# A trunk's last activation pair, first gate weights and final gate in another order

## The chip, the cores and the metric

One core of one Trainium2 chip. The metric is the device time of the whole program in microseconds (us). The engines are TensorE (PE, with its weight loads as PEld), VectorE (DVE), ScalarE (ACT), GpSimd (POOL) and SyncE (SP), which issues most of the DMAs. Each engine works its instructions in the order in which they stand in the program, and waits on semaphores where an instruction needs what another engine or a DMA made.

## The reference, cut to what matters

Two layers over 512 tokens of width 1024. Each layer has a token mixer (not touched here), a squared-ReLU MLP and a gated per-layer embedding; a last norm follows.

```python
for i in range(DEPTH):                     # DEPTH = 2
    hn = rmsnorm(h, norm_mix_g[i])
    h = h + mixer(hn)                      # even: stick-breaking + differential; odd: dilated windows
    hn = rmsnorm(h, norm_mlp_g[i])
    u = jnp.square(jax.nn.relu(hn @ w_mlp_up[i]))
    h = h + u @ w_mlp_down[i]
    gate = jax.nn.sigmoid(rmsnorm(h, norm_ple_g[i]) @ w_ple_gate[i])
    h = h + (p[i] @ w_ple_proj[i]) * gate
return rmsnorm(h, final_norm_g)
```

## The kernel before

**Products.** Every fp32 operand is split into a high part, written by ACT as fp32r (`wh`, `hi`, `uh`), and a low part, the rest, written by DVE or POOL (`wl`, `lo`, `ul`). A product is three matmuls: high by high, high by low, low by high (`mm3`, lines 137 to 142). h is kept transposed in eight tiles of 128 x 512.

**Weights.** `wload` has SP bring 1 MB into `raw` (two buffers), `wsplit` makes the two parts of half a load (128 x 1024 each, lines 117 to 129) in a ring of three buffers, or four in a pool that is handed in. A load can start only when both halves of the load before last have been split.

**The MLP** (line 711). `up(ch, c)` makes two accumulators of 24 matmuls each (512 columns), then for the pair: relu times norm on DVE (L738), square on ACT (L739), three differences on DVE (L744 to L748), and the split of all seven quarters `u` into `uh` (L750) and `ul` (L751), since the down product is done by a scheme with seven products of half size. In the last chunk of four an additional split of one quarter goes to `spare` (L742, L743). `down(ch, c)` makes sums of the weight's quarters (`s13`, `s24`), splits them (L789, L790), and runs its products over the four pairs k = 0 to 3. The first down unit of the last chunk, `down(3, 0)`, takes k = 0 to 2 of all its products ahead of k = 3, as pair 3 comes last. Its weight splits are w13, w24, w11 and, inside the products, w for A12 and A22.

The side sums of a unit (L888) read what a POOL DMA has accumulated (`side`). `nxt.done(k)` then scales and splits an h tile for the gate's norm and adds its squares to `rstd`: by DVE (L254), or for the first tiles by an accumulating DMA of POOL's (L247). `down_last(3)` is the last down unit, in plain form: two accumulators of 36 matmuls.

**The gate.** In layer 0 `ple_t` (line 915) takes four loads of `w_gate`, each with two blocks; for the first load it alternates the two accumulators over k. In layer 1 `ple_final` (line 933) works in two halves of the columns, each with four weight blocks b = 0 to 3 from two loads, and four token tiles t. In the first half b is the outer loop, with the transposes of h between (`turn`, L943, DVE's copies L944) and the norm: `norm.finish()` sums `rstd` over the partitions by two matmuls (L261, L262), then Ln (L210) and Exp (L213) on ACT, three steps on DVE (L214 to L216), four transposes (L284) and `rcol` (L286). In the second half t is outer. Each tile has a sigmoid (L994), product (L995), addition (L996) and the sum of squares (L997); after the first half POOL multiplies by the final norm's weights (L999). After a tile's second half, thirteen small DVE steps (L1003 to L272) make its scale; ACT (L950) and DVE (L952) apply it and SP writes the tile out.

**What sets the order.** The program's text gives a priority, and a scheduler places the instructions of each engine by it and by its own costs, so that each engine's order differs from the text. `order(later, earlier)` (line 224) binds two instructions without a semaphore of its own.

## Time and profile before

| | us |
|---|---|
| median of three runs | 1305.18 |
| lowest, highest | 1303.14, 1307.39 |
| the profiled execution, own time | 1305.36 |
| its span, first to last instruction | 1303.6 |
| PE busy in the span | 1277.1 (98%) |
| DVE, ACT, POOL busy | 1005.1, 710.2, 213.2 |
| granted TensorE clock, mean | 0.996 |

Times in the rows below count from the first instruction; layer 0 ends near 640. A matmul row's end is modelled and overlaps the next one's start, so the spacing of the starts is its cost. A waiting instruction shows in brackets how long its engine was idle ahead of it, and who released it. A row that ends in x2 or x3 is several instructions in one stretch.

### The profile page before, as it was taken

To read this page: it belongs to the slowest core of one execution; us is meant where nothing else is said; L and a number is where in the kernel's file an instruction comes from. 1 tells how busy PE (TensorE), PEld (TensorE's weight loads), DVE (VectorE), ACT (ScalarE), POOL (GpSimd) and SP (SyncE) were. 2 spreads that over 40 slices of the span, in tenths; PEclk is the share of its full clock that TensorE was granted. 3 is DMA by queue.
4 is the path that set the end of the run, shared out by engine and by line. 5 is a ranking of instruction groups with operands and counts; after the bars stand their busy time and mean duration, and the time that the engine had idled before them with its cause. 6 is when DMAs were issued, how large, how long until landed. Compare 5 with 4: busy or idle time off the path is not lost.

```text
span 1303.6 us, 19326 instructions
## 1 busy us (share of the span) xinstructions
PE 1277.1 (98%) x7520; PEld 1125.7 (86%) x7520; DVE 1005.1 (77%) x1673; ACT 710.2 (54%) x1149; POOL 213.2 (16%) x184
## 2 busy tenths in 40 slices
PE   9999999999999999999999999999999999999996
PEld 7988887888988989988889888788899898998975
DVE  6788798778858869679767777887785885976876
ACT  6666867555535344355456666764553433534644
POOL 2433533400000000001023333231000000000201
PEclk9999999999999999999999999999999999999998
DMA  6421423222232322646432222212323133254741
GB/s 213 140 81 61 151 74 113 89 98 97 98 99 96 117 103 77 189 116 172 173 130 82 81 89 82 65 58 97 101 94 129 65 103 124 85 163 141 170 145 65
DMA packets 33996, 144.25 MB, mean 111 GB/s; under 512 B 3889, under 2 KB 4625, under 8 KB 21233
## 3 DMA queue, kind: packets, MB, share of 16 engines
q1 hardware_dynamic: 29680, 135.16, 30.6%
q0 software_dynamic: 4224, 7.87, 3.5%
q8 instruction: 59, 0.97, 0.3%
q14 instruction: 33, 0.26, 0.1%
HBM read 131.92 MB, written 6.37 MB: 106 GB/s over the span
## 4 chain that ended last, share of the span: by engine, by line
PE 76%; DVE 11%; ACT 5%; DMA 4%; issue 3%; POOL 0%; SPq 0%; ACTq 0%; DVEq 0%; POOLq 0%
PE mm L138 11%; PE mm L142 10%; PE mm L141 10%; PE sc L141 5%; PE sc L142 5%; PE sc L138 5%; PE pv L142 4%; PE pv L141 4%; PE pv L138 4%; PE tp L142 4%; PE tp L141 4%; PE tp L138 4%; PE pv L558 3%; PE tp L539 2%; DMA side<-u 2%
## 5 line engine op out<-in xcount | busy, mean ns | idle before, releaser
L122 ACT ACTIVATE wh<-raw 128x1024 fp32r<-128x1024 f32 (+1 forms) x156 | 160.5, 1034 | 142.7 <-PE mm L141 47.9
L126 POOL TENSOR_TENSOR wl<-raw,wh 128x512 fp32r<-128x512 f32 (+1 forms) x132 | 178.3, 1373 | 304.1 <-ACT wh L122 304.1
L138 PE MATMUL mm<-hi,wh 128*128 128x512 f32 x472 | 187.1, 396 | 0.2 <-ACT pjt L372 0.2
L142 PE MATMUL mm<-hi,wl 128*128 128x512 f32 x472 | 185.0, 392 | 1.6 <-DVE wl L128 1.5
L141 PE MATMUL mm<-lo,wh 128*128 128x512 f32 x472 | 184.6, 391 | 0.0
L128 DVE TENSOR_TENSOR wl<-raw,wh 128x1024 fp32r<-128x1024 f32 x90 | 109.4, 1221 | 46.4 <-ACT wh L122 40.8
L142 PEld LDWEIGHTS mm<-hi,wl 128*128 128x128 f32 x472 | 88.6, 188 | 22.2 <-DVE wl L128 2.2
L138 PEld LDWEIGHTS mm<-hi,wh 128*128 128x128 f32 x472 | 88.7, 188 | 16.8 <-ACT pjt L372 0.4
L141 PEld LDWEIGHTS mm<-lo,wh 128*128 128x128 f32 x472 | 88.8, 188 | 15.6
L760 POOL DMA_DIRECT2D s<-in_w_down_dram x4 | 4.5, 1123 | 579.1 <-DMA s<-in_w_down_dram 313.2
L789 ACT ACTIVATE wh<-s 128x1024 fp32r<-128x1024 f32 x58 | 61.1, 1053 | 52.8 <-DVE s L776 14.7
L751 DVE TENSOR_TENSOR ul<-u,uh 128x1792 fp32r<-128x1792 f32 x32 | 64.8, 2024 | 31.9 <-ACT uh L750 31.8
L533 ACT ACTIVATE e<-e,mn 128x128 f32<-128x128 f32 (+3 forms) x96 | 53.8, 561 | 62.3 <-DVE mn L530 61.9
L790 DVE TENSOR_TENSOR wl<-s,wh 128x1024 fp32r<-128x1024 f32 x58 | 70.8, 1221 | 13.9 <-ACT wh L789 13.5
L750 ACT ACTIVATE uh<-u 128x1792 fp32r<-128x1792 f32 x32 | 54.5, 1703 | 48.4 <-DVE u L748 48.2
L739 ACT ACTIVATE u<-u 128x512 f32<-128x512 f32 x64 | 39.7, 626 | 68.0 <-DVE u L738 67.8
L141 PE MATMUL sc<-lo,wh 128*128 128x512 f32 x184 | 72.1, 392 | 0.3 <-DVE lo L183 0.3
L138 PE MATMUL sc<-hi,wh 128*128 128x512 f32 x184 | 72.2, 392 | 0.1
L142 PE MATMUL sc<-hi,wl 128*128 128x512 f32 x184 | 71.9, 391 | 0.0
L138 PE MATMUL mm<-wh,hi 128*128 128x256 f32 (+1 forms) x216 | 63.2, 292 | 0.0
L142 PE MATMUL mm<-wh,lo 128*128 128x256 f32 (+1 forms) x216 | 62.9, 291 | 0.0
L141 PE MATMUL mm<-wl,hi 128*128 128x256 f32 (+1 forms) x216 | 62.8, 291 | 0.0
(305 smaller groups left out, 3887.1 us busy)
## 6 DMA issues: line engine op xcount, KB each, us to landing
raw<-in_w_up_dram SPq DMA_DIRECT2D x32, 1024.0 KB, 4.9
raw<-in_w_down_dram SPq DMA_DIRECT2D x32, 1024.0 KB, 4.9
raw<-in_w_in_dram SPq DMA_DIRECT2D x23, 1024.0 KB, 4.9
raw<-in_w_gate_dram SPq DMA_DIRECT2D x8, 1024.0 KB, 6.0
bias<-urow SPq DMA_DIRECT2D x24, 256.0 KB, 3.6
raw<-in_w_outa_dram SPq DMA_DIRECT2D x8, 768.0 KB, 4.2
pj<-pjd SPq DMA_DIRECT2D x16, 256.0 KB, 5.7
h<-in_xT_dram SPq DMA_DIRECT2D x8, 256.0 KB, 5.7
```

The lines of the kernel that those rows point to most:

```text
L122: nc.scalar.activation(hi, src, AF.Copy)
L126: nc.gpsimd.tensor_tensor(lo[:, kx], src[:, kx], hi[:, kx].bitcast(F32), op=ALU.subtract)
L128: nc.vector.tensor_tensor(lo, src, hi.bitcast(F32), op=ALU.subtract)
L138: mm = nc.tensor.matmul(acc, lh, rh, start=start, stop=False)
L141: nc.tensor.matmul(acc, lh, rl, start=False, stop=False)
L142: return mm.ins, nc.tensor.matmul(acc, ll, rh, start=False, stop=stop).ins
L533: nc.scalar.activation(e[:, 0:n], e[:, 0:n], AF.Exp, scale=-1.0, bias=mn, accum_out=s)
L739: nc.scalar.activation(ui, ui, AF.Square, scale=0.5)
L750: nc.scalar.activation(uh, u, AF.Copy)
L751: part = nc.vector.tensor_tensor(ul, u, uh.bitcast(F32), op=ALU.subtract)
L789: nc.scalar.activation(hi, src, AF.Copy)
L790: low[:] = [nc.vector.tensor_tensor(lo, src, hi.bitcast(F32), op=ALU.subtract).ins]
```

## The change

It has three parts.

1. In `down(3, 0)` of both layers, the low part of w24 is bound behind the last pair's first relu, the high part of A12/A22 behind its second square, and that block's low part behind its last difference.
2. In `down_last` the first load of the gate is asked for, and split, after the first accumulator's matmuls in the text. The side sums of the unit before are bound behind the first block's low part, and the `rstd` additions of its two tiles behind the second's. `ple_t` and `ple_final` take these blocks over.
3. In `ple_final` the fourth block of the first half comes from the pool handed in, not the ring, and the last block of the second half from the ring. The high and low parts of the last load are bound behind the norm's Exp and its last step. `tok_cols` stands later, after the second token tile of b = 3.

```diff
 def wsplit(raw, i, nk, n, pool=None):
...
-            nc.vector.tensor_tensor(lo, src, hi.bitcast(F32), op=ALU.subtract)
+            last_low[:] = [nc.vector.tensor_tensor(lo, src, hi.bitcast(F32), op=ALU.subtract).ins]
+        last_high[:] = [act.ins]
...
 def rsqrt(...):
+        root[:] = [ex.ins, nc.vector.scalar_tensor_tensor(y, t, 3.0 / scale, y, op0=ALU.subtract, op1=ALU.mult).ins]
...
 Norm.stats:
+                add = nc.vector.tensor_tensor(self.acc, self.acc, sq, op=ALU.add)
+                for a in late_add:
+                    order(add.ins, a)
...
 up:
+                chain.append(nc.vector.scalar_tensor_tensor(ui, acc, 0.0, rstd[0], op0=ALU.max, op1=ALU.mult).ins)
+                chain.append(nc.scalar.activation(ui, ui, AF.Square, scale=0.5).ins)
...
-            hidden[ch, c] = (uh, ul, part.ins)
+            hidden[ch, c] = (uh, ul, part.ins, chain[0], chain[3], t4.ins)
...
 down:
             w24 = split(s24)
+            if last and c == 0:
+                order(low[0], hidden[ch, 3][3])
...
                     w = split(rv[:, A12:A22 + 1])
+                    if last and c == 0:
+                        order(high[0], hidden[ch, 3][4])
+                        order(low[0], hidden[ch, 3][5])
...
 down_last:
-            low.clear()
             defer = []
-            finished(c - 1)
...
+                if i == 0:
+                    raw = wload(w_gate[layer, 0])
+                    n = (KT, P) if layer < DEPTH - 1 else (2, 512)
+                    gate.append(wsplit(raw, 0, *n))
+                    low[:] = last_low
+                    gate.append(wsplit(raw, 1, *n))
+                    late_add[:] = last_low
+                    finished(c - 1)
...
 ple_t:
-            blk = block(w_gate[layer, c], KT, P)
+            blk = gate if c == 0 else block(w_gate[layer, c], KT, P)
...
 ple_final:
-            gw = []
-            for half in range(2):
+            gw = [] if c else list(gate)
+            for half in range(1 - c, 2):
                 raw = wload(w_gate[layer, 2 * c + half])
                 for b in range(2):
-                    gw.append(wsplit(raw, b, 2, 512, pool=fpool if c else None))
+                    gw.append(wsplit(raw, b, 2, 512, pool=None if (c, half, b) in ((0, 1, 0), (1, 1, 1)) else fpool))
+                    if c and half:
+                        order(last_high[0], root[0])
+                        order(last_low[0], root[1])
...
                         contract(t, b, 0)
+                        if b == 3 and t == 1:
+                            rcol = tok_cols(rstd)
...
-                        rcol = tok_cols(norm.finish())
+                        rstd = norm.finish()
                         turn(1)
```

The diff as printed is cut and its hunks are named by function. How the scheduler placed the instructions shows in each engine's order. Line numbers of the changed kernel are its own.

**DVE at the end of the last `up` of layer 1.** `u_11905` is the last pair, `wl_11946` the low part of w24, `wl_11999` that of A12/A22. Before:

```order
L790 TENSOR_TENSOR wl_11946<-s_2147_11930,wh_11945 128x1024
L738 SCALAR_TENSOR_TENSOR u_11905<-pv_11855,rstd_9229 128x512
L743 TENSOR_TENSOR spare_11753<-u_11905,spare_11753 128x256
L738 SCALAR_TENSOR_TENSOR u_11905<-pv_11856,rstd_9229 128x512
L790 TENSOR_TENSOR wl_11999<-raw_11927,wh_11998 128x1024
L744 TENSOR_TENSOR u_11905<-u_11905 128x2x256
L746 SCALAR_TENSOR_TENSOR u_11905<-u_11905 128x256
L748 SCALAR_TENSOR_TENSOR u_11905<-u_11905 128x256
L751 TENSOR_TENSOR ul_11907<-u_11905,uh_11906 128x1792
```

In the changed kernel, the same stretch of DVE:

```order
L748 SCALAR_TENSOR_TENSOR u_11905<-pv_11855,rstd_9229 128x512
L800 TENSOR_TENSOR wl_11946<-s_2147_11930,wh_11945 128x1024
L753 TENSOR_TENSOR spare_11753<-u_11905,spare_11753 128x256
L748 SCALAR_TENSOR_TENSOR u_11905<-pv_11856,rstd_9229 128x512
L754 TENSOR_TENSOR u_11905<-u_11905 128x2x256
L756 SCALAR_TENSOR_TENSOR u_11905<-u_11905 128x256
L758 SCALAR_TENSOR_TENSOR u_11905<-u_11905 128x256
L800 TENSOR_TENSOR wl_11999<-raw_11927,wh_11998 128x1024
L761 TENSOR_TENSOR ul_11907<-u_11905,uh_11906 128x1792
```

Each low part moved down, past one relu and past the three differences. On ACT the high part of A12/A22 moved behind the second square; layer 0 reads the same.

**DVE around the last down unit of layer 0.** `side_3071` and `side_3072` are the sums of the third unit, `wl_6195` and `wl_6199` (before) or `wl_6100` and `wl_6104` (now) the gate's first two low parts. Before:

```order
L888 TENSOR_TENSOR side_3071<-side_3071,side_3072 128x256
L128 TENSOR_TENSOR wl_6195<-raw_6192,wh_6194 128x1024
L888 TENSOR_TENSOR h_97<-h_97,side_3071 128x256
...
L254 TENSOR_TENSOR rstd_5902<-rstd_5902,e_6072 128x512
L873 TENSOR_TENSOR h_99<-h_99,tp_6082 128x512
L183 SCALAR_TENSOR_TENSOR lo_6076<-h_98,gcols,hi_6075 128x512
L254 TENSOR_TENSOR rstd_5902<-rstd_5902,e_6079 128x512
L183 SCALAR_TENSOR_TENSOR lo_6121<-h_99,gcols,hi_6120 128x512
L128 TENSOR_TENSOR wl_6199<-raw_6192,wh_6198 128x1024
```

In the changed kernel, from the same place of DVE on:

```order
L128 TENSOR_TENSOR wl_6100<-raw_6097,wh_6099 128x1024
L910 TENSOR_TENSOR h_97<-h_97,side_3072 128x256
L910 TENSOR_TENSOR side_3071<-side_3071,side_3072 128x256
...
L894 TENSOR_TENSOR h_99<-h_99,tp_6060 128x512
L128 TENSOR_TENSOR wl_6104<-raw_6097,wh_6103 128x1024
L261 TENSOR_TENSOR rstd_5902<-rstd_5902,e_6119 128x512
L186 SCALAR_TENSOR_TENSOR lo_6123<-h_98,gcols,hi_6122 128x512
```

The first low part moved up past the first two side sums, the second past both `rstd` additions and two `lo`. In layer 1 both moved alike.

**ACT in the final gate.** `raw_12686` and `raw_12696` are the third and fourth load, `rstd_12174` the norm. Before:

```order
L259 ACTIVATE e_12595<-rstd_12174 128x512
L122 ACTIVATE wh_12688<-raw_12686 128x1024
L122 ACTIVATE wh_12490<-raw_12484 128x1024
L122 ACTIVATE wh_12692<-raw_12686 128x1024
L122 ACTIVATE wh_12698<-raw_12696 128x1024
L122 ACTIVATE wh_12702<-raw_12696 128x1024
L210 ACTIVATE rstd_12174<-tp_12594,eps_n 128x512
L213 ACTIVATE rstd_12174<-rstd_12174 128x512
```

In the changed kernel, on ACT:

```order
L122 ACTIVATE wh_12688<-raw_12686 128x1024
L122 ACTIVATE wh_12692<-raw_12686 128x1024
L268 ACTIVATE e_12595<-rstd_12174 128x512
L213 ACTIVATE rstd_12174<-tp_12594,eps_n 128x512
L216 ACTIVATE rstd_12174<-rstd_12174 128x512
L122 ACTIVATE wh_12698<-raw_12696 128x1024
L122 ACTIVATE wh_12702<-raw_12696 128x1024
```

Ln and Exp (the two rows that write `rstd`) moved up past the two high parts of the fourth load; the three others moved ahead of the norm.

**DVE in the final gate's second half.** `fin_12741` and `fin_12742` are the first tile's scale, `gt_12784` and `ht_12477` belong to the second tile. Before:

```order
L272 SCALAR_TENSOR_TENSOR fin_12741<-fin_12742,fin_12741 128x1
L952 SCALAR_TENSOR_TENSOR ht_12466<-ht_12466,fin_12741,gb_12464 128x512
L995 TENSOR_TENSOR gt_12784<-gt_12784,pj_12458 128x512
L996 TENSOR_TENSOR ht_12467<-ht_12467,gt_12784 128x512
L1003 TENSOR_TENSOR fin_12789<-ssq_12471 128x1
```

In the changed kernel, on DVE (four small steps of the scale and the first tile's last step follow):

```order
L281 SCALAR_TENSOR_TENSOR fin_12741<-fin_12742,fin_12741 128x1
L1023 TENSOR_TENSOR gt_12784<-gt_12784,pj_12468 128x512
L279 TENSOR_TENSOR fin_12742<-fin_12741 128x1
L1024 TENSOR_TENSOR ht_12477<-ht_12477,gt_12784 128x512
L280 SCALAR_TENSOR_TENSOR fin_12742<-fin_12742,fin_12740 128x1
```

The second tile's product and addition moved from behind the first tile's scaling to the middle of its small steps; on ACT the second tile's sigmoid moved ahead of the first tile's scaled copy. Ahead of this stretch, `rcol` moved on DVE behind all four copies of the second `turn` and behind the first low part of the fourth load, where it stood ahead of the copies and behind both low parts before.

More of the change, by code (lines that the diff above doesn't have):

```diff
@@ L121, in wsplit @@
         src = raw[:, i * nk * n:(i + 1) * nk * n].rearrange("p (k c) -> p k c", k=nk)
-        nc.scalar.activation(hi, src, AF.Copy)
+        act = nc.scalar.activation(hi, src, AF.Copy)
         if lo_eng[0] is nc.gpsimd:
@@ L127, in wsplit @@
         else:
-            nc.vector.tensor_tensor(lo, src, hi.bitcast(F32), op=ALU.subtract)
+            last_low[:] = [nc.vector.tensor_tensor(lo, src, hi.bitcast(F32), op=ALU.subtract).ins]
+        last_high[:] = [act.ins]
         return hi, lo
+    last_low, last_high = [], []
     def block(src, nk, n):
@@ L212, in rsqrt @@
             order(ln.ins, tables)
-        nc.scalar.activation(y, y, AF.Exp, scale=-0.5)
+        ex = nc.scalar.activation(y, y, AF.Exp, scale=-0.5)
         nc.vector.tensor_tensor(t, y, y, op=ALU.mult)
         nc.vector.scalar_tensor_tensor(t, mean, eps / scale, t, op0=ALU.add, op1=ALU.mult)
-        nc.vector.scalar_tensor_tensor(y, t, 3.0 / scale, y, op0=ALU.subtract, op1=ALU.mult)
+        root[:] = [ex.ins, nc.vector.scalar_tensor_tensor(y, t, 3.0 / scale, y, op0=ALU.subtract, op1=ALU.mult).ins]
+    root = []
     def use_tables(after):
@@ L228, in order @@
             reason="activation tables")
+    late_add, gate = [], []
     class Norm:
@@ L253, in stats @@
             else:
-                nc.vector.tensor_tensor(self.acc, self.acc, sq, op=ALU.add)
+                add = nc.vector.tensor_tensor(self.acc, self.acc, sq, op=ALU.add)
+                for a in late_add:
+                    order(add.ins, a)
         def finish(self, tables=None):
@@ L715, in mlp @@
         sides = [[fpool.tile([P, S], F32, tag=f"side{x}{c}", name=nm("side"), bufs=1) for x in range(2)] for c in range(4)]
-        hidden, spare, stages, b12, low, lows = {}, [], [], [], [], []
+        hidden, spare, stages, b12, low, lows, high = {}, [], [], [], [], [], []
         def up(ch, c):
@@ L735, in up @@
             ul = fpool.tile([P, 7, HW], F32R, tag="ul", name=nm("ul"), bufs=5)
+            chain = []
             for i, acc in enumerate(accs):
                 ui = u[:, B11 + 2 * i:B11 + 2 * i + 2].rearrange("p a c -> p (a c)")
-                nc.vector.scalar_tensor_tensor(ui, acc, 0.0, rstd[0], op0=ALU.max, op1=ALU.mult)
-                nc.scalar.activation(ui, ui, AF.Square, scale=0.5)
+                chain.append(nc.vector.scalar_tensor_tensor(ui, acc, 0.0, rstd[0], op0=ALU.max, op1=ALU.mult).ins)
+                chain.append(nc.scalar.activation(ui, ui, AF.Square, scale=0.5).ins)
             if ch == NCH - 1:
@@ L747, in up @@
                 u[:, T2], u[:, T1], -1.0, u[:, B22], op0=ALU.mult, op1=ALU.subtract)
-            nc.vector.scalar_tensor_tensor(
+            t4 = nc.vector.scalar_tensor_tensor(
                 u[:, T4], u[:, T2], -1.0, u[:, B21], op0=ALU.mult, op1=ALU.subtract)
@@ L788, in split @@
                 src = src.rearrange("p s (k c) -> p s k c", k=4)
-                nc.scalar.activation(hi, src, AF.Copy)
+                high[:] = [nc.scalar.activation(hi, src, AF.Copy).ins]
                 low[:] = [nc.vector.tensor_tensor(lo, src, hi.bitcast(F32), op=ALU.subtract).ins]
@@ L872, in down_last @@
                                                  stop=k == KT - 1 and lh is wl)
+                if i == 0:
[6 more added lines that the diff above has]
+                    finished(c - 1)
                 nc.vector.tensor_tensor(h[2 * c + i], h[2 * c + i], acc, op=ALU.add)
                 nxt.done(2 * c + i, defer=defer)
+            late_add.clear()
         def finished(c):
@@ L921, in ple_t @@
             if c == 0:
+                gate.clear()
                 rstd = norm.finish()
```

## The prediction

> **What bounds the kernel now.** I read the page's chain of work first, then the list of what TensorE (PE) waited for, then the timelines of single engines around those waits.
>
> ```profile
> PE 76%; DVE 11%; ACT 5%; DMA 4%; issue 3%; POOL 0%; SPq 0%; ACTq 0%; DVEq 0%; POOLq 0%
> ...
> PE mm L141 <- DVE ul L751: 2.0, 2, 1.0
> PE tp L284 <- DVE rstd L216: 1.7, 1, 1.7
> ...
> PE mm L142 <- DVE wl L128: 1.5, 1, 1.5
> ```
>
> Three quarters of the chain is matmul, so a microsecond in which PE stands still is a microsecond of the kernel, as long as PE stays the bound afterwards. The list (total, times, longest) names few waits: PE waits for VectorE (DVE) or ScalarE (ACT), and no row of it names a DMA. The change touches three rows: `ul` of the last activation pair (once per layer), the gate's low part (layer 0), and the gate norm's `rstd` (layer 1). The last 35 us are different: there PE is not the bound, see the third part.
>
> **Part 1, the last activation pair (both layers).** Layer 1, DVE first, then ACT, then PE, and PE in layer 0; start, duration, operation, and idle time with its releaser in brackets:
>
> ```profile
> 1195.39 1.22 DVE L790 TENSOR_TENSOR wl<-s,wh 128x1024 fp32r<-128x1024 f32 x1
> 1196.53 0.69 DVE L738 SCALAR_TENSOR_TENSOR u<-pv,rstd 128x512 f32<-128x512 f32 x1
> 1198.42 0.43 DVE L743 TENSOR_TENSOR spare<-u,spare 128x256 fp32r<-128x256 f32 x1 [1.21 <-ACT spare L742]
> ...
> 1199.37 1.23 DVE L790 TENSOR_TENSOR wl<-raw,wh 128x1024 fp32r<-128x1024 f32 x1
> 1200.51 0.69 DVE L744 TENSOR_TENSOR u<-u 128x512 f32<-128x512 f32 x1
> ...
> 1203.94 2.02 DVE L751 TENSOR_TENSOR ul<-u,uh 128x1792 fp32r<-128x1792 f32 x1 [1.83 <-ACT uh L750]
> ```
>
> ```profile
> 1197.97 0.42 ACT L742 ACTIVATE spare<-u 128x256 fp32r<-128x256 f32 x1
> 1198.29 1.04 ACT L789 ACTIVATE wh<-raw 128x1024 fp32r<-128x1024 f32 x1
> 1199.48 0.63 ACT L739 ACTIVATE u<-u 128x512 f32<-128x512 f32 x1
> 1202.21 1.70 ACT L750 ACTIVATE uh<-u 128x1792 fp32r<-128x1792 f32 x1 [2.10 <-DVE u L748]
> ```
>
> ```profile
> 1204.70 0.28 PE L138 MATMUL mm<-uh,wh 128*128 128x256 f32 x1
> 1206.03 0.39 PE L141 MATMUL mm<-ul,wh 128*128 128x256 f32 x1 [1.04 <-DVE ul L751]
> ```
>
> ```profile
> 578.42 0.39 PE L141 MATMUL mm<-ul,wh 128*128 128x256 f32 x1 [0.93 <-DVE ul L751]
> ```
>
> The pair's chain is relu, square, differences, `uh`, `ul`. Two low parts (1.22 and 1.23 us) and one high part (1.04) stand in it. With the new order the first relu takes the place at 1195.39; its square runs 1196.17 to 1196.80 while DVE does the low part (to 1197.2); ACT's `spare` ends at 1197.25, DVE's at 1197.7; the second relu ends at 1198.3, its square at 1199.0. Before, that square ended at 1200.11 and the difference then stood behind a low part until 1200.51; now the difference starts at 1199.05. From there to the start of `ul` the rows give 3.43 us (1200.51 to 1203.94): `ul` starts at 1202.5 and ends at 1204.5, 1.46 earlier.
>
> PE wants it 0.12 (the spacing of its 256-column matmuls, 0.28 less the overlap) after 1204.70, at 1204.82. So the whole wait goes, with 0.3 to spare. It cost 1206.03 - 1204.82 = 1.2, and one stretched matmul (0.39 for 0.28) 0.1 more: **1.3 us in layer 1**, and by its idle time 0.11 less, **1.2 us in layer 0**. What is late next: the low part of A12/A22 moves behind the differences, from 1199.37 to about 1200.6, ending 1201.8. 63 matmuls of 0.12 stand ahead of 1204.70 in its unit, which so starts at 1197.15; PE needs the part in the 48th: 1202.8. That leaves 1.0 us. It also frees `raw` 1.2 us later, but the load into it is for the unit after next, more than a whole unit of matmuls away. Bounds: 0 if the wait only changes its name, 2.5 for both layers together. I take 2.5, since the slack on both sides is from rows of the same operations.
>
> **Part 2, the gate's first weights (layer 0).** DVE, then PE:
>
> ```profile
> 605.95 0.42 DVE L888 TENSOR_TENSOR h<-h,side 128x256 f32<-128x256 f32 x1 [2.37 <-DMA side<-u]
> ...
> 606.62 1.22 DVE L128 TENSOR_TENSOR wl<-raw,wh 128x1024 fp32r<-128x1024 f32 x1
> ...
> 611.45 0.69 DVE L254 TENSOR_TENSOR rstd<-rstd,e 128x512 f32<-128x512 f32 x1 [0.72 <-DMA rstd<-side]
> ...
> 614.58 1.22 DVE L128 TENSOR_TENSOR wl<-raw,wh 128x1024 fp32r<-128x1024 f32 x1
> ```
>
> ```profile
> 613.99 0.40 PE L141 MATMUL mm<-lo,wh 128*128 128x512 f32 x1
> 615.85 0.50 PE L142 MATMUL mm<-hi,wl 128*128 128x512 f32 x1 [1.46 <-DVE wl L128]
> ```
>
> Both low parts are placed by the new order ahead of what DVE waits for: the first before the side sums (2.37 us of idle time hide its 1.22), the second before the `rstd` addition that waits for an accumulating DMA. The second then runs at about 610.1 to 611.3: the side sums lose the low part in their midst (1.1 earlier), and its high part on ACT follows them. PE needs it at 614.2. The wait goes: 615.85 - 614.22 (0.23 is the spacing at 512 columns) = 1.63, and 0.1 of stretched matmul, **1.7 us**. Behind the second low part now queue the additions and `lo` of three h tiles, 1.2 us at most; PE reads those 7 to 10 us after its gate begins (six matmuls of 0.23 a k, from the sixth k on), so nobody waits. In layer 1 the same move removes no wait of PE (none is in the list), but lets `raw` go about 5 us sooner, and with it the third load of the gate. Bounds 0 and 1.8; I take 1.7.
>
> **Part 3, the final gate (layer 1).**
>
> ```profile
> 1253.41 0.66 PE L943 MATMUL tp<-ident,h 128*128 128x128 f32 x4 [0.20 <-DVE ht L944]
> ...
> 1259.39 0.40 PE L261 MATMUL tp<-e,ones_r 128*128 128x512 f32 x1
> ...
> 1265.45 0.63 PE L284 MATMUL tp<-ident,rstd 128*128 128x128 f32 x4 [1.74 <-DVE rstd L216]
> ...
> 1291.60 0.28 PE L142 MATMUL mm<-wh,lo 128*128 128x256 f32 x1
> ```
>
> ```profile
> 1223.87 19.57 SPq L114 DMA_DIRECT2D raw<-in_w_gate_dram  x3
> ...
> 1259.80 2.01 ACT L122 ACTIVATE wh<-raw 128x1024 fp32r<-128x1024 f32 x2 [8.68 <-DMA raw<-in_w_gate_dram]
> 1261.71 0.67 ACT L210 ACTIVATE rstd<-tp,eps_n 128x512 f32<-128x512 f32 x1
> ...
> 1284.20 0.67 ACT L994 ACTIVATE gt<-tp,rcol 128x512 f32<-128x512 f32 x1
> ...
> 1295.02 0.45 ACT L994 ACTIVATE gt<-mm,rcol 128x256 f32<-128x256 f32 x1
> ```
>
> ```profile
> 1266.12 0.16 DVE L286 TENSOR_SCALAR rcol<-tp 128x4 f32<-128x4 f32 x1 [0.81 <-PE tp L284]
> ...
> 1271.99 1.52 DVE L995 TENSOR_TENSOR gt<-gt,pj 128x512 f32<-128x512 f32 x1 [0.18 <-ACT gt L994]
> ...
> 1279.53 0.69 DVE L996 TENSOR_TENSOR ht<-ht,gt 128x512 f32<-128x512 f32 x1
> ...
> 1281.01 0.16 DVE L1003 TENSOR_TENSOR fin<-ssq 128x1 f32<-128x1 f32 x1 [0.79 <-ACT gt L997]
> ...
> 1283.32 0.16 DVE L272 SCALAR_TENSOR_TENSOR fin<-fin,fin 128x1 f32<-128x1 f32 x1
> ...
> 1291.74 0.69 DVE L996 TENSOR_TENSOR ht<-ht,gt 128x512 f32<-128x512 f32 x1
> ```
>
> ```profile
> 1271.33 3.34 POOL L999 TENSOR_TENSOR ht<-ht,gb 128x512 f32<-128x512 f32 x2 [36.29 <-ACT gt L997]
> ```
>
> Now the norm's Ln stands on ACT behind two high parts that wait for the fourth gate load until 1259.80. PE loses 1.74 for it, and 0.3 at the first transposes. With Ln and Exp ahead of the weights, PE begins its second half about 2.0 earlier. But PE is not the bound there: its last matmul ends at 1291.9, and the last sigmoid starts at 1295.02. So the end must be followed on ACT and DVE, in four steps.
> (i) Ln can start when the two sums of L261/L262 are done: 1259.39 - 0.3 + 0.24 + 0.4, near 1259.8; Exp ends at 1261.1. On DVE follow, in the new order, three steps of the norm and three more copies out of PSUM between them (0.69 each), one low part (1.22), then `rcol`: 1261.1 + 6 x 0.69 + 1.22 less the overlaps (0.08 each, as between neighbouring rows) is near 1266.2, no earlier than 1266.12 before.
> (ii) The copies are done by then, so the products for the four token tiles run closer together; POOL's multiplications fall on them. The first tile of the second half is added by 1279.65 where it was 1280.22: 0.6 gained.
> (iii) From there to the third tile's addition, 1292.43 - 1280.22 = 12.2 before, two rounds of square and reading its sum (0.8), thirteen small steps (1281.01 to 1283.48, 0.19 each, 2.5 together), ACT's scaled copy, sigmoid (0.67), product and addition (0.69 each) one after another. In the new order the second tile's sigmoid stands ahead of that copy, and its product and addition inside the small steps: 0.8 + 7 small steps 1.35 + product and addition with two steps 1.4 + the rest 1.0 + DVE's L952 0.75 + 2.5 + 0.75 + 0.69 + 0.69 = 9.9, some 9.7 with overlaps. 2.5 gained.
> (iv) From there the orders of ACT and DVE are equal, and PE (end 1289.9) stays ahead of the last sigmoid (1291.9).
> That makes **3.1 us**. Bounds: 0.6 if (iii) gives nothing; 2.0 + 3.1 = 5.1, if the end hung on PE alone.
>
> The row to weigh is POOL's. Its two multiplications take 3.34; the DVE product that begins 0.66 after them takes 1.52, where the same operation without POOL takes 0.69. By the rows DVE waits out the POOL operation in progress, and (ii) counts it so at all four of them, some 0.8 us each but for the third.
>
> [...]
>
> **Sum.** 1.3 + 1.2 + 1.7 + 3.1 = 7.3 us. The profiled execution took 1305.36 and would take 1298.1; the median shown is 1305.18, 0.18 less, so I forecast **1297.9**. Instructions and bytes stay the same in number. The gate's blocks in other buffers cost nothing that I count: the fourth block no longer waits for the buffer of the first, the last one takes that buffer long after PE has read it, and the transfers that PE and ACT now check for have landed by then (DVE's additions that read them stand ahead of the last h tile).
>
> **Rivals.**
> (A) *The end keeps its old pace*: ACT and DVE stay the bound and step (iii) does not come, as a late sigmoid there pushes the small steps back. For it: the second tile's product stands between steps that other tiles wait for. Against: its sigmoid needs only PE, and PE is 2 us ahead. It gives 4.2 + 0.6, so 1300.4.
> (B) *The wait changes its name in part 1*: PE waits for the A12/A22 low part instead of `ul`. For it: that part starts only after the differences. Against: 1.0 us of slack. The price is 2.5: 1300.4.
> (C) *The gains of layer 0 are lost later*, to something paced by transfers, and the end keeps its pace as well. Against: no DMA in PE's list. 7.3 - 2.9 - 2.5 = 1.9: 1303.3.
> (D) *Slower*: `rcol`, which all sigmoids need, now stands on DVE behind the low part that waits for the fourth gate load. That load landed by 1259.80; now it goes out some 5 us sooner, close behind the third (1 MB), `pj` (2 MB) and `gb` (0.5 MB). It has until 1261.1, the end of Exp; each us later delays the end by one, and beyond 1268.4 the kernel is slower than before.
>
> ```profile
> DMA packets 33996, 144.25 MB, mean 111 GB/s; under 512 B 3889, under 2 KB 4625, under 8 KB 21233
> ```
>
> The third load was issued at 1243.1 (the end of SP's stretch of three, less its 0.33) and goes out near 1237.8 now. At the mean rate of this line the 4.5 MB from there on would take 40 us, to 1278, and the kernel 1315. But the same 4.5 MB went from 1243.1 to 1259.8 before, 16.7 us; at that pace they end at 1254.5.
>
> **How the numbers follow.** Forecast 0.66, (A) 0.14, (B) 0.07, (C) 0.08, (D) 0.05. A measurement of this kernel tells about 0.3% (3.9 us) from no change. Faster by more, below 1301.3: forecast, (A) and (B), less 0.07 for those that a scatter of some us takes over the line: 0.80. Within 0.3%: 0.15. Slower: 0.05. The range of 1295.0 to 1302.0 takes in the forecast with its upper bound (1295.9 less some scatter), (A) and (B), 0.87 less the scatter; (C) and (D) are out.
>
> **What would show it.** Part 1: in both layers no wait of PE for `ul`, and `ul` starting about 1.4 sooner against PE's unit; a wait for `wl` of the same unit in its place is (B). Part 2: no wait for the gate's low part near 614. Part 3: Ln before the last two high parts, no wait for `rstd`, 9.7 us instead of 12.2 between the additions of the first and the third tile, and the last sigmoid some 2 us after PE's end instead of 3.1. Wrong would be: `rcol` later than 1.5 us behind its old place against the gate's start, a PE wait that is new, or a final stage no shorter than before.

## The result, and the profile after

| | before | changed |
|---|---|---|
| median of six runs, us | 1305.07 | 1297.96 |
| lowest, highest | 1303.14, 1307.39 | 1296.67, 1298.60 |
| the profiled execution, own time | 1305.36 | 1297.82 |
| its span | 1303.6 | 1296.1 |
| granted TensorE clock, mean | 0.996 | 0.997 |

The ratio is 0.9943, with a 95% interval of 0.9930 to 0.9956: 7 us faster, forecast 1297.9. Two more measurements of the same kernel, beside the experiments, gave 0.9924 (0.9912 to 0.9937) and 0.9934 (0.9920 to 0.9947). The medians of the changed kernel stay within 1297.1 to 1298.0; those of the kernel before go from 1305.1 to 1306.7, so the gain is 7.1, 9.5 or 8.9 us by the runs that it is set against.

What TensorE waited for in the changed kernel (engine, line, releaser: total, times, longest): a row that has grown, then the one that is left of those quoted before:

```profile
PE sc L144 <- DVE lo L186: 0.9, 3, 0.4
PE mm L144 <- DVE ul L761: 0.2, 1, 0.2
```

The rows for `rstd`, for the gate's low part and for the first transposes of the final gate are gone. `ul` is left with 0.2 of 2.0. The `lo` row, 0.3 once before, lies in the first 14 us, ahead of anything that was changed.

**Part 1.** TensorE in layer 0, then in layer 1 (start, duration, operation, idle time and releaser in brackets):

```profile
577.60 0.28 PE L144 MATMUL mm<-ul,wh 128*128 128x256 f32 x1
...
1202.44 0.28 PE L141 MATMUL mm<-uh,wh 128*128 128x256 f32 x1
1202.95 0.39 PE L144 MATMUL mm<-ul,wh 128*128 128x256 f32 x1 [0.23 <-DVE ul L761]
```

In layer 0 `ul` is in time; in layer 1 0.23 is left. DVE of layer 1 shows why, from a load on; the first row is the kernel before, the others are the changed one:

```profile
1179.09 0.69 DVE L777 TENSOR_TENSOR s<-s,raw 128x512 f32<-128x512 f32 x1 [0.80 <-DMA raw<-in_w_down_dram]
```

```profile
1177.30 0.69 DVE L787 TENSOR_TENSOR s<-s,raw 128x512 f32<-128x512 f32 x1 [1.28 <-DMA raw<-in_w_down_dram]
...
1191.67 2.03 DVE L761 TENSOR_TENSOR ul<-u,uh 128x1792 fp32r<-128x1792 f32 x1 [1.83 <-ACT uh L760]
1193.80 0.69 DVE L748 SCALAR_TENSOR_TENSOR u<-pv,rstd 128x512 f32<-128x512 f32 x1
1194.41 1.22 DVE L800 TENSOR_TENSOR wl<-s,wh 128x1024 fp32r<-128x1024 f32 x1
...
1200.87 2.03 DVE L761 TENSOR_TENSOR ul<-u,uh 128x1792 fp32r<-128x1792 f32 x1 [0.69 <-ACT uh L760]
```

The order is the one wanted: relu, then the low part. But TensorE comes to this place 2.26 us earlier than before (1204.70 to 1202.44), while DVE's first addition waits for a load and comes only 1.79 earlier (1179.09 to 1177.30).

**Part 2.** DVE in layer 0, then TensorE at the place of the old wait:

```profile
602.57 1.23 DVE L128 TENSOR_TENSOR wl<-raw,wh 128x1024 fp32r<-128x1024 f32 x1
...
608.24 1.22 DVE L128 TENSOR_TENSOR wl<-raw,wh 128x1024 fp32r<-128x1024 f32 x1
615.80 0.69 DVE L261 TENSOR_TENSOR rstd<-rstd,e 128x512 f32<-128x512 f32 x1 [6.34 <-DMA rstd<-side]
...
620.07 0.74 DVE L186 SCALAR_TENSOR_TENSOR lo<-h,gcols,hi 128x512 fp32r<-128x512 f32 x1
```

```profile
613.30 0.39 PE L145 MATMUL mm<-hi,wl 128*128 128x512 f32 x1
...
621.91 0.39 PE L144 MATMUL mm<-lo,wh 128*128 128x512 f32 x1
```

Both low parts are early and TensorE does not wait at 613.3. Behind them DVE stood 6.34 us for the accumulating transfer, where it had 0.72 before; the last `lo` ended at 620.81, and TensorE read it at 621.91. That is 1.1 us from a new wait. What made the transfer so slow in this trace stays open.

**Part 3.** TensorE, ACT and DVE in the final gate:

```profile
1261.40 0.63 PE L293 MATMUL tp<-ident,rstd 128*128 128x128 f32 x4
...
1286.36 0.28 PE L145 MATMUL mm<-wh,lo 128*128 128x256 f32 x1
```

```profile
1256.53 0.69 ACT L213 ACTIVATE rstd<-tp,eps_n 128x512 f32<-128x512 f32 x1 [11.18 <-PE tp L271]
...
1276.00 0.67 ACT L1022 ACTIVATE gt<-tp,rcol 128x512 f32<-128x512 f32 x1
...
1279.73 0.72 ACT L973 ACTIVATE ht<-ht,fin 128x512 f32<-128x512 f32 x1 [0.19 <-DVE fin L281]
...
1287.50 0.46 ACT L1022 ACTIVATE gt<-mm,rcol 128x256 f32<-128x256 f32 x1
```

```profile
1262.90 0.15 DVE L295 TENSOR_SCALAR rcol<-tp 128x4 f32<-128x4 f32 x1
...
1267.97 2.40 DVE L1023 TENSOR_TENSOR gt<-gt,pj 128x512 f32<-128x512 f32 x2 [1.38 <-ACT gt L1022]
...
1273.68 1.66 DVE L1024 TENSOR_TENSOR ht<-ht,gt 128x512 f32<-128x512 f32 x1
...
1284.23 0.69 DVE L1024 TENSOR_TENSOR ht<-ht,gt 128x512 f32<-128x512 f32 x1
```

Ln waits for TensorE's sums alone, and TensorE no longer for `rstd` (1261.40). The second tile's sigmoid (1276.00) stands ahead of the first scaled copy (1279.73). The first and third tile's additions end at 1275.34 and 1284.92: 9.6 us apart, where before had 12.2. The last sigmoid starts 0.9 us after TensorE's end (1286.64), before 3.1.

### The profile page after: what moved, and what is told of

The parts are those of the page before. It is cut to its first block, busy times and chain, and to the rows that moved or that the text cites. A ratio compares the mean times of both kernels' runs of the same rounds, so it can differ in the third digit from the quotient of the medians.

```text
span 1296.1 us, 19322 instructions
## 1 busy us (share of the span) xinstructions
PE 1276.5 (98%) x7520; PEld 1124.8 (87%) x7520; DVE 1004.2 (77%) x1673; ACT 709.5 (55%) x1149; POOL 213.0 (16%) x184
## 4 chain that ended last, share of the span: by engine, by line
PE 80%; DVE 9%; ACT 4%; DMA 3%; issue 2%; POOL 0%; SPq 0%; ACTq 0%; DVEq 0%; POOLq 0%
PE mm L141 11%; PE mm L145 11%; PE mm L144 10%; PE sc L144 5%; PE sc L145 5%; PE sc L141 5%; PE pv L145 4%; PE pv L144 4%; PE pv L141 4%; PE tp L145 4%; PE tp L144 4%; PE tp L141 4%; PE pv L567 3%; PE tp L548 2%; PE sc L522 1%
```

## The experiments

They were measured in three groups (e1 to e4, e5 to e8, e9 to e12), each with runs of the kernel before beside it: medians 1306.54, 1306.62 and 1306.71. Line numbers shift a little between kernels; the operation names the place.

### The parts one by one

The first three kernels are the one before with one part of the change each.

Part 1 alone (e1):

```diff
+            if last and c == 0:
+                order(low[0], hidden[ch, 3][3])
...
+                        order(high[0], hidden[ch, 3][4])
+                        order(low[0], hidden[ch, 3][5])
```

> Before with part 1 alone (the orders around the last activation pair). My theory, by the two traces: the waits of TensorE for ul (0.93 in layer 0, 1.04 in layer 1) were worth their idle time and no more, so layer 0 gives 0.93 and layer 1 0.8 to 1.04 (0.23 is left where the down load of that stretch lands late), 1.7 to 2.0 us in all, near 1303.3. The sum on record had 2.5 for it (1302.6). Rival (B), the wait changes its name: no gain, 1305, and a wait for wl in the same unit. Rival (C), lost later: the waits are gone and the end stays at 1305.

Measured: 1304.86, before 1306.54; ratio 0.9982 (0.9971 to 0.9992). The size is as expected, 1.7 to 2.4 us, but the trace is not. TensorE in layer 0, behind part 1, and its clock there (stretch, length, busy, granted clock, DMA share, GB/s):

```profile
615.76 0.79 PE L145 MATMUL mm<-hi,wl 128*128 128x512 f32 x1 [2.46 <-DVE wl L128]
616.35 0.63 PE L141 MATMUL mm<-hi,wh 128*128 128x512 f32 x1
616.78 0.63 PE L144 MATMUL mm<-lo,wh 128*128 128x512 f32 x1
```

```profile
616.00:620.00 4.00, 4.00 (x12) 0.61 0.72 267
```

Both waits for `ul` are gone. But the gate's low part comes from DVE when it did before, so TensorE, which is there 1 us sooner, waits 2.46 instead of 1.46. The gain of layer 0 is eaten at the next wait: rival (C) in small, paced by DVE. And behind this wait the clock is granted at half: matmuls are 0.43 apart instead of 0.23. This execution is the slowest of the twelve (1306.13); how many of the others had the half clock was not shown. In layer 1 the gain of 0.9 stays. In the final gate the first transposes wait 1.70 instead of 0.20 and `rstd` 0.43 instead of 1.74, about the same in sum.

Part 2 alone (e2):

```diff
+                if i == 0:
+                    raw = wload(w_gate[layer, 0])
...
+                    low[:] = last_low
+                    gate.append(wsplit(raw, 1, *n))
+                    late_add[:] = last_low
+                    finished(c - 1)
```

> Before with part 2 alone (the gate's first load and its low parts ahead of the side sums and of the rstd additions). My theory: 1.5 to 1.7 us, all of it at the wait for wl near 614 in layer 0, so 1303.5. It should also show VectorE waiting some 6 us for the accumulating transfer into rstd (0.72 before), since the third load of the gate now goes out beside it, with no wait of TensorE for it. Rival: that long wait comes from the sum of all parts, and alone stays below 2 us. Rival (C): the gain is lost later and the time stays at 1305.

Measured: 1302.86; ratio 0.9970 (0.9958 to 0.9982). Twice what was expected, 3.7 us. The long DVE wait is a miss as well: 0.88 here. Where the rest came from, on ACT in the final gate:

```profile
1253.81 2.01 ACT L122 ACTIVATE wh<-raw 128x1024 fp32r<-128x1024 f32 x2 [5.22 <-DMA raw<-in_w_gate_dram]
1259.28 0.69 ACT L213 ACTIVATE rstd<-tp,eps_n 128x512 f32<-128x512 f32 x1 [3.46 <-PE tp L271]
```

The fourth load has landed by 1253.81, where it landed by 1259.80 before, so its high parts are done ahead of Ln, without part 3. TensorE's 1.74 for `rstd` is gone.

Part 3 alone (e3):

```diff
-                    gw.append(wsplit(raw, b, 2, 512, pool=fpool if c else None))
+                    gw.append(wsplit(raw, b, 2, 512, pool=None if (c, half, b) in ((0, 1, 0), (1, 1, 1)) else fpool))
+                    if c and half:
+                        order(last_high[0], root[0])
+                        order(last_low[0], root[1])
...
+                        if b == 3 and t == 1:
+                            rcol = tok_cols(rstd)
```

> Before with part 3 alone (the final gate's buffers, the two bindings, rcol four contractions later). My theory, by the two traces: 3.5 to 4.3 us, so 1301.2, with 9.6 us between the additions of the first and the third tile (12.2 before). The sum on record had 3.1 (1302.1). Rival: part 3 needs the earlier third and fourth load that part 2 brings; then rcol comes later by the late landing of the fourth load, and the gain is under 2 us.

Measured: 1308.58; ratio 1.0010 (0.9996 to 1.0024). Expected was a gain of at least 3.5. The scheduler, with this text, puts the first transposes of `turn` ahead of the gate's first matmul, and TensorE waits there for an h tile:

```profile
1243.86 0.60 PE L953 MATMUL tp<-ident,h 128*128 128x128 f32 x4
1247.13 0.55 PE L953 MATMUL tp<-ident,h 128*128 128x128 f32 x3 [2.67 <-DVE h L883]
1247.77 0.71 PE L141 MATMUL mm<-wh,hi 128*128 128x512 f32 x2
```

From here to the norm's sums TensorE needs 23.1 us, where the kernel before needed 18.6 (1240.79 to 1259.39):

```profile
1266.91 0.40 PE L270 MATMUL tp<-e,ones_r 128*128 128x512 f32 x1
```

These 4.5 us are mostly the wait and the half clock behind it (0.61 granted over 1248 to 1252), and the shorter end gives 4.0 back. In layer 0 this trace loses another 2.5: the wait for the gate's low part is 2.30 instead of 1.46, again with half clock behind it (0.57 granted over 617 to 621), at a place that part 3 does not touch. So this kernel does not price part 3; the kernels below do.

The fourth kernel (e4) keeps the change but puts `rcol` back to its old place:

```diff
-                        if b == 3 and t == 1:
-                            rcol = tok_cols(rstd)
...
-                        rstd = norm.finish()
+                        rcol = tok_cols(norm.finish())
```

> The change with rcol's transposes and reading put back where they stood (behind the norm, ahead of the second four transposes); buffers and bindings as in the change. My theory: it is this place that lets the order around the small steps come out differently, so the additions of the first and the third tile are 12.2 us apart again and the end is 2.5 to 3.1 us later than with the change: 1300.5 to 1301.1, rival (A) of the prediction carried out. Rival: the earlier Ln alone makes the gain; then 9.6 us stay and the time is within 0.6 of 1298.0.

Measured: 1301.16; ratio 0.9953 (0.9934 to 0.9971), which is 5.4 below the runs of the kernel before beside it. Against the three medians of the change (1297.11 to 1297.96) it is 3.2 to 4.1 us slower. In its trace the additions of the first and third tile end at 1276.75 and 1288.95, 12.2 us apart, the old pace. The direction is the one of the theory; the size is over its 3.1. In the traces the last sigmoid stands 3.7 us behind TensorE's end where the change has 0.9, which is 2.8; another 0.9 was lost near 840 us, far ahead of the edit, where this execution ran at half the clock for a while (0.72 granted over 840 to 846) and the first trace of the change did not (1.00). Whether that is the rest of the medians' difference was not shown.

### What part 3 is worth, and which piece of it

The change once more (e5):

> The change itself once more, for a comparison on the same chip and a second trace. By the ratio measured before (0.9943) some 7.4 us below the kernel before. My theory that its remaining waits are all under 1.4 us has the runs within 2 us of each other, where the kernel before spread over 8. In layer 1 the wait for ul should be 0 to 0.4, depending on when the down load of that stretch lands.

Measured: 1297.11 (1296.98 to 1297.97), ratio 0.9924: 9.5 us below the kernel before, not 7.4, and the runs within 1 us of each other. The wait for `ul` in layer 1 was 0.17 in this trace, and DVE did not wait for the accumulating transfer at all.

Without part 3 (e6): the lines of e3's diff taken out again, so that buffers, bindings and `rcol` are as before.

> The change without part 3 (buffers, bindings and rcol's place of the final gate as before). My theory now, from the trace of part 2 alone: the earlier third and fourth load of part 2 already bring Ln in time, so there is no wait of TensorE for rstd here; what part 3 brings is the order around the small steps (9.6 instead of 12.2 us between the additions of the first and the third tile), less some 0.4 for rcol, which part 3 holds up. So 2.2 us slower than the change. Rival, as the sum on record had it: Ln's place comes from part 3; then the wait of 1.7 for rstd is back and the kernel is 3.1 us or more slower than the change.

Measured: 1299.68, ratio 0.9945 (0.9932 to 0.9957), 2.6 us over the change of the same group. ACT, then DVE:

```profile
1250.66 2.01 ACT L122 ACTIVATE wh<-raw 128x1024 fp32r<-128x1024 f32 x2 [5.52 <-DMA raw<-in_w_gate_dram]
1255.81 0.69 ACT L213 ACTIVATE rstd<-tp,eps_n 128x512 f32<-128x512 f32 x1 [3.14 <-PE tp L271]
```

```profile
1273.55 0.69 DVE L1019 TENSOR_TENSOR ht<-ht,gt 128x512 f32<-128x512 f32 x1
...
1285.76 0.69 DVE L1019 TENSOR_TENSOR ht<-ht,gt 128x512 f32<-128x512 f32 x1
```

Ln is in time without part 3, so the rival of the record falls. What is missing is the pace: 12.2 us between the two additions.

Without the bindings alone (e7):

```diff
-                    if c and half:
-                        order(last_high[0], root[0])
-                        order(last_low[0], root[1])
```

> The change without its two bindings of the last high and low parts. My theory: the fourth load has landed near 1251, ScalarE and VectorE are idle then (11.2 and 5.0 us), so the four operations go there and rcol comes 0.8 to 1.1 us earlier (near 1262.0); but the order then has the second tile's product behind all thirteen small steps, so the additions of the first and the third tile are some 10.6 us apart instead of 9.6, and the time is that of the change within 0.5. Rival, what the bindings were said to do: without them Ln stands behind the high parts that wait for the load, the wait for rstd is back, and the kernel is 1.7 to 2 us slower.

Measured: 1297.54, ratio 0.9928 (0.9914 to 0.9942), 0.4 over the change. ACT, then DVE:

```profile
1251.45 2.01 ACT L122 ACTIVATE wh<-raw 128x1024 fp32r<-128x1024 f32 x2 [5.54 <-DMA raw<-in_w_gate_dram]
...
1256.43 0.69 ACT L213 ACTIVATE rstd<-tp,eps_n 128x512 f32<-128x512 f32 x1 [2.96 <-PE tp L271]
```

```profile
1261.96 0.16 DVE L295 TENSOR_SCALAR rcol<-tp 128x4 f32<-128x4 f32 x1 [0.21 <-PE tp L293]
...
1272.45 1.66 DVE L1021 TENSOR_TENSOR ht<-ht,gt 128x512 f32<-128x512 f32 x1
...
1283.93 0.69 DVE L1021 TENSOR_TENSOR ht<-ht,gt 128x512 f32<-128x512 f32 x1
```

`rcol` comes 0.9 earlier, the additions end 10.5 us apart, and Ln waits for nothing but TensorE: gain and loss cancel as expected. The bindings protect nothing here; the load landed by 1251.45.

Then the order of the tail alone (e9), on parts 1 and 2 with the final gate as before. `gated(t, i)` is the old text of a tile's matmuls, sigmoid, product, addition and square; tile t + 1 now stands ahead of tile t's small steps. The pair handed to `rsqrt_cols` binds the second Newton step behind the next tile's product and addition, the one handed to `finish` the scaled copy behind its sigmoid and the scaling behind its addition:

```diff
+            gated(0, 0)
             for t in range(QT):
...
+                if not last:
+                    sg, pr, ad, sq_a = gated(t + 1, 0)
+                    ahead = sg, ad
+                if t == QT - 2:
+                    sg, _, ad, _ = gated(t + 1, 1)
+                    order(sq_a.ins, sg.ins)
...
-                    rsqrt_cols(r, m, w)
+                    rsqrt_cols(r, m, w, (pr, ad) if t == 0 else ())
...
-                    finish(*done.pop())
+                    finish(*done.pop(), ahead)
```

> Parts 1 and 2 with the final gate as before (no new buffers, no bindings, rcol early), and in place of part 3 the order of its tail written out: the next tile's sigmoid ahead of the scaled copy, its product and addition inside the first tile's small steps, and two more of the kind (the third tile's product ahead of the second tile's scaling, the last sigmoid ahead of the square before it). My theory, part 3 is worth its tail order and nothing else: 9.3 to 9.6 us between the additions of the first and the third tile, the last sigmoid within 0.3 of TensorE's end (3.1 us behind it with parts 1 and 2 alone, 0.9 with the change), so 2.6 to 3.2 us faster than parts 1 and 2 and 0.3 to 0.7 faster than the change. Rival: buffers, bindings or rcol's place carry part of it; then it stays 1 us or more slower than the change.

Measured: 1296.96, ratio 0.9927 (0.9915 to 0.9940). It is 0.8 below the change of the same group (e10, next), and as fast as anything here that computes the whole result, though the intervals of the two ratios overlap. DVE, then ACT:

```profile
1274.75 0.69 DVE L1020 TENSOR_TENSOR ht<-ht,gt 128x512 f32<-128x512 f32 x1
...
1283.53 0.69 DVE L1020 TENSOR_TENSOR ht<-ht,gt 128x512 f32<-128x512 f32 x1
```

```profile
1287.22 0.47 ACT L1018 ACTIVATE gt<-mm,rcol 128x256 f32<-128x256 f32 x1 [1.88 <-PE mm L145]
```

The additions are 8.8 us apart, and the last sigmoid waits for TensorE, 0.1 after its end. The buffers, the bindings and the later `rcol` are not needed for any of it.

The change a third time (e10):

> The change a third time, for comparison on the same chip: 7.4 to 9.5 us below the kernel before (the two ratios so far, 0.9943 and 0.9924), its runs within 2 us of each other.

Measured: 1297.79 (1297.62 to 1298.93), ratio 0.9934, as expected.

Parts 1 and 3 (e12), the lines of e2's diff taken out of the change:

> The change without part 2. My theory, part 2 is what lets the others count: without it TensorE waits for the gate's low part in layer 0 2.3 to 2.5 us instead of 1.46, since part 1 only brings it there sooner, and runs at half its clock for some 3 us behind that wait; the earlier end of part 3 gives about that back. The sum of the two parts alone (1.7 faster, 2.0 slower) is +0.3, so 1305 to 1308 where the kernel before has 1306.6. Rival, the parts add up as on record (1.3 + 1.2 + 3.1): 5.6 us faster than before.

Measured: 1307.03, ratio 0.9998 (0.9987 to 1.0009). The time is the expected one, but by another way, so that is luck. TensorE waited 2.34 us for the gate's low part in layer 0, as expected, which takes back the 0.8 that part 1 had given there; the half clock behind it did not come (1.00 granted over 616 to 620). In layer 1 it waited 2.82 in the early transposes, which the scheduler places here as in e3, and ran at half the clock from there for nearly seven us (columns as in e1: the granted clock is 0.52):

```profile
1243.00:1250.00 7.00, 6.16 (x19) 0.52 0.99 346
```

From the gate's first transpose to the norm's sums it needs 24.1 us, 5.5 more than the kernel before. So the zero is mostly the price of that order, and what parts 1 and 3 are worth without part 2 and without that order was not shown.

### GpSimd's multiplications beside DVE's operations

GpSimd's multiplication left out of the change (e8, the first line alone), and cut in four (e11):

```diff
-                    nc.gpsimd.tensor_tensor(hk[t][:, 0:512], hk[t][:, 0:512], gb[:, 0:512], op=ALU.mult)
+                    for x in range(0, 512, 128):
+                        nc.gpsimd.tensor_tensor(hk[t][:, x:x + 128], hk[t][:, x:x + 128], gb[:, x:x + 128], op=ALU.mult)
```

> The change with GpSimd's four multiplications by the final norm's weights left out (the first half of each output row is then not multiplied by them). My theory: VectorE's long operations (2.40 for two, 1.66) fall to 0.69 each, the first tile of the second half is added 1.7 to 2.1 us earlier, but the end then hangs on TensorE, whose last matmul ends 0.8 us ahead of the last sigmoid, so it gains only 0.5 to 0.8 us. [...] Rival (the figure on record): the end is 2 us earlier.

Measured: 1296.71, ratio 0.9919 (0.9905 to 0.9932), 0.4 below the change of the same group, a little less than expected. DVE, then ACT:

```profile
1267.97 1.29 DVE L1023 TENSOR_TENSOR gt<-gt,pj 128x512 f32<-128x512 f32 x2 [1.38 <-ACT gt L1022]
...
1272.57 0.69 DVE L1024 TENSOR_TENSOR ht<-ht,gt 128x512 f32<-128x512 f32 x1
```

```profile
1286.73 0.47 ACT L1022 ACTIVATE gt<-mm,rcol 128x256 f32<-128x256 f32 x1 [0.24 <-PE mm L145]
```

The same operations take 1.29 for 2.40, from the same start, and 0.69 for 1.66. The first tile is added 2.1 us earlier (1273.26 for 1275.34), the last sigmoid only 0.8: then TensorE is the bound.

> The change with each of GpSimd's four multiplications (1.5 us for 512 columns) written as four of 128 columns; the result is the same. My theory, VectorE waits out one GpSimd operation in progress and no more: its long operations (2.40 for two and 1.66, 2.1 more than without GpSimd) lose most of their excess, 0.8 or less is left, and the first tile of the second half is added 1.2 us earlier or more; the end, which then hangs on TensorE, is 0.3 to 0.7 earlier. [...]

Measured: 1296.99, ratio 0.9926 (0.9913 to 0.9938), 0.8 below the change of the same group (e10). DVE, then GpSimd:

```profile
1268.61 1.58 DVE L1023 TENSOR_TENSOR gt<-gt,pj 128x512 f32<-128x512 f32 x2 [1.38 <-ACT gt L1022]
1270.11 1.82 DVE L1024 TENSOR_TENSOR ht<-ht,gt 128x512 f32<-128x512 f32 x2
...
1274.09 0.84 DVE L1024 TENSOR_TENSOR ht<-ht,gt 128x512 f32<-128x512 f32 x1
```

```profile
1267.47 9.45 POOL L1028 TENSOR_TENSOR ht<-ht,gb 128x128 f32<-128x128 f32 x16 [32.36 <-ACT gt L1025]
```

GpSimd now takes 9.45 us instead of 6.0, yet DVE loses about 1.1 instead of 2.1 (0.3, 0.54 and 0.15 in these rows, 0.07 in the product between them). So, as the theory has it, DVE loses less where one GpSimd operation is shorter (1.51 us for a whole one, 0.63 on average for a quarter); no other lengths were measured. The sizes are a little off: 0.8 or less of excess was expected, and the first tile is added 1.0 earlier against the gate's start than in e10, not 1.2.

## Why the prediction was right, point by point

The time was right to 0.1 us, and the sum of the trace is 7.5 where 7.3 was forecast. It is right by its sum more than by its terms: 0.5 and 0.3 too much was forecast for parts 1 and 2 and 1.2 too little for the final gate, and that these nearly cancel is luck. The gains by TensorE's own starts, before against after:

| term | forecast | trace |
|---|---|---|
| part 1, layer 0 | 1.2 | 1.2 |
| part 1, layer 1 | 1.3 | 0.8 |
| part 2, layer 0 | 1.7 | 1.75, 0.35 lost again at the norm |
| up to the first tile's addition | 0.6 | 1.7 |
| first to third addition | 2.5 | 2.6 |

The rest is small: 0.1 lost in the first 17 us and 0.2 in layer 0 by 509, both ahead of anything that was changed, and 0.1 gained on the way to the final gate.

- **Part 1** was right in its mechanism and in layer 0. In layer 1 the step "`ul` starts at 1202.5" missed by 0.63 (1200.87, on the old scale 1203.13): 0.47 because the load at 1177.30 did not come forward as far as TensorE did, 0.18 because the relu starts 0.10 after `ul`'s end where I let it overlap by 0.08. My 0.3 of slack did not cover that. Over the fourteen traces the wait is 0 to 0.45 where part 1 is in, 0.9 to 1.4 where it isn't.
- **Part 2** was right in layer 0. "1.2 us at most" for what queues behind the second low part was wrong in one trace: 6.34 of waiting, which cost TensorE 0.35 at the norm and left 1.1 us to spare at the last `lo`; in the nine other traces with part 2 the same wait is 0 to 1.4. For layer 1 I wrote that it removes no wait of TensorE. It does: e2 and e6 show that the earlier third and fourth load bring Ln in time.
- **Part 3** was sized 3.1 and the final gate gave 4.3, but not all of it by part 3. From the gate's first matmul to the first tile's addition it took 39.4 us before, 37.4 with parts 1 and 2 alone (e6) and 37.8 with the change: the 1.7 of the table are 2.0 by part 2, less 0.4 that part 3 costs. "With Ln and Exp ahead of the weights" is what part 2 does already (e6), and the bindings are worth nothing (e7). What part 3 adds is step (iii), the pace of the tail, 2.6 forecast as 2.5 and shown by itself in e6 and e9; against that, it delays `rcol`. Step (i) was right (`rcol` no earlier than before, against the gate's start). Step (ii) was mis-sized by 1.1: 0.5 of it is GpSimd, which I let hold DVE up at all four multiplications (2.55 in all, my estimate from the rows of 3.34 and 1.52) where it did so twice, for 2.1 in all; 0.6 is there without GpSimd too (e8 adds the first tile at 1276.5 on the old scale, where 1279.65 less those 2.55 is 1277.1), and which step gives it stays open. By the same 1.1 the last sigmoid stands 0.9 behind TensorE's end, not some 2.
- **The sum** assumed that the parts add. In layer 0 they do not: part 1's gain there is lost at the next wait unless part 2 takes that wait away (e1, e12). By the times alone it is not decided: parts 1 and 2 gave 1.7 and 3.7 us alone and 6.9 together (e6), which agrees within the scatter, and part 3 alone (-2.0) and parts 1 and 3 (0) carry the other order of the scheduler, 4.5 and 5.5 us in their traces.
- **The rivals.** (A), the old pace at the end, is what the kernel does without the new order (e4, e6), 2.6 to 4.1 slower than the change; I had 2.5. (B) did not come: no wait for `wl` took the place of `ul`'s. (C) is real without part 2 in layer 0 (e1), but the pace there came from DVE, not from a transfer. (D) did not come: the fourth load went out at 1243.0, and the nearest trace that waits for it (e7) has it by 1251.45, 8 us after its issue, against a deadline near 1258 on the new scale.
- **GpSimd beside DVE.** That DVE loses time there is borne out: without GpSimd's operations DVE's rows fall from 2.40 and 1.66 to 1.29 and 0.69 (e8), and beside quarters DVE loses about 1.1 instead of 2.1 (e11). How GpSimd's operations make DVE's longer was not shown. The upper bound on record, 1295.9 with the end on TensorE alone, took the whole 2 us for the end; no run shows them, and e8 shows 0.4 to 0.8, since TensorE is the bound from there.

How much of the scatter of the kernel before (1303.1 to 1311.7 over its 61 runs, where the change has 1296.7 to 1298.9 in 17) comes from waits with half clock behind them was not shown: none of its long executions was traced.

## What to carry to other kernels

Waits on one engine stand in series: taking one away makes the next one longer if that is paced by another engine (1.46 to 2.46 us in e1), so look at what paces the next wait before adding gains up, and test edits together as well as alone. A scheduler may also answer an edit with another order elsewhere, as in e3 and e12, and then the time doesn't price the edit. Where several engines share a tail, the order of the short steps can be worth more than any duration (12.2 us between two additions in e6, 8.8 in e9), and can be bound directly instead of being left to fall out of another edit. A weight load that goes out sooner moves the later loads of that buffer, and its gain may turn up at a place where the list of waits names an activation: in e2 the fourth load landed by 1253.81, by 1259.80 before, and the wait of 1.74 for `rstd` was gone.

## What the runs showed of the hardware

Behind four waits of 2.3 to 2.8 us TensorE's granted clock fell to half: in e1 behind 2.46 (0.61 granted over 616 to 620), in e3 behind 2.30 (0.57 over 617 to 621) and 2.67 (0.61 over 1248 to 1252), which makes 3.1 to 3.4 us at half each time, and in e12 at and behind 2.82 (0.52 over seven us). In layer 0 of e1 and e3 that cost 1.6 us beyond the wait. Behind 2.34 in e12 it kept its full clock (1.00 over 616 to 620). Half clock also came behind two waits of 1.27 and 0.51 that lie 0.5 us apart near 840, in four traces of fourteen (e2, e4, e9 and the change in e10), and cost 0.8 to 0.9; e2 beside the first trace of the change, with nearly the same two waits (1.25 and 0.51):

```profile
840.00:846.00 6.00, 5.88 (x21) 0.72 0.00 0
```

```profile
840.00:846.00 6.00, 6.00 (x32) 1.00 0.00 0
```

The same two waits have half clock behind them in one run and full clock in another, and what decides that was not shown. Two waits of 1.8 together cost up to 0.9 us beyond their length here, single ones of 2.30 and 2.46 cost 1.6, one of 2.34 nothing.
